# Forgetting attention: a hand-over to dense blocks before the values' product

## The chip, the cores and the metric

The kernel runs on one core of a Trainium2 chip. The metric is the device time of one execution in microseconds (us); lower is better. TensorE multiplies matrices, VectorE and ScalarE do elementwise work, GpSimd fills constants, and SyncE issues the transfers of weights from HBM.

## The reference, cut to what matters

A trunk of four layers over 272 positions (16 learned meta tokens and 256 real ones), model width 1024. Layers 0 and 3 mix tokens by forgetting attention, layer 1 by gated linear attention, layer 2 by a gated delta rule; each is followed by a dense SwiGLU network of inner width 2816. All inputs are float32. The forgetting attention has 16 heads of 64:

```python
def fox_attend(q, cq, qpos, k, v, ck, kpos):
    s = jnp.einsum('bqhd,bkhd->bhqk', q, k).astype(jnp.float32)
    bias = cq[..., :, None] - ck[..., None, :]
    mask = kpos[None, :] <= qpos[:, None]
    s = jnp.where(mask, s + bias, -jnp.inf)
    p = jax.nn.softmax(s, axis=-1)
    return jnp.einsum('bhqk,bkhd->bqhd', p.astype(v.dtype), v)
```

Its output is multiplied by a sigmoid gate and by an output matrix of 1024x1024.

## The kernel before

**Dense products.** Activations lie transposed, features on partitions and the 272 positions along the free axis. Every weight matrix is cut into blocks of 128x128, eight blocks to a unit of 128x1024. `make_unit` (line 573) loads a unit, lets ScalarE write its rounded high part `wh` and VectorE the rest `wl`. `block` (line 551) computes one block's share of an output as three matmuls in float32r: `zh,wh`, `zh,wl`, `zl,wh` (in the output projection `oh`, `ol`; in the dense network `ah`, `al`). An output of 128 features is a `Dense`, an accumulator in one of the eight PSUM banks; at most three are open while a mixer runs.

**The planner.** The order of all instructions is worked out while the program is built. `Trunk` keeps a clock of its own, `now`, advanced by estimated costs. Tasks are Python generators: a task that yields a tile, or a tuple of tiles, is taken up again when the plan's time of the last of these plus `LAT` (0.14 us) has come; one that yields an event waits until it is set; one that needs a PSUM bank asks for it every 0.1 us of the plan. `turn` (line 470) takes the first task that is due; if none is, `step` (line 506) places one dense block whose unit is split and whose accumulator is open. TensorE executes strictly in the order in which the planner placed its work. A matmul placed before its operands are there by the plan moves the plan's clock forward (line 403); on the chip the engine waits. The ScalarE and VectorE work has planned slots too, and is ordered by them. The plan halves TensorE's speed after a thin stretch; it looks at that in fixed ticks of its clock.

**Forgetting attention** (`fox`, line 828). Its dense outputs come in this order: the forget gate; then for each of four groups of two head pairs the queries, keys and values; then the eight gates. A generator `attend(jp)` (line 932) treats a pair of heads, `hh` = 0 and 1:

1. It waits for the scores' inputs and for the event of the pair before, and takes four banks (`pa`, `pb` for each head).
2. It places the bias product (`cs,sel`) and the scores (`raw`) in three tiles of queries (96, 96 and 80 positions), then the softmax on VectorE and ScalarE, which ends in the normalised `pr`.
3. It yields on `pr[0]`, transposes the first head's `pr` on TensorE (six transposes, `con,pr` in the rows, line 424) into a bank `pt` and a corner of `pb`, and copies them out: ScalarE writes `pts` (96x448), VectorE `pt2` (80x80). It yields on `pr[1]` and does the same for the second head.
4. It takes a bank `po` and places the values' product: `vsb` against `pts` and `pt2` of both heads, the two heads in different columns of the array. ScalarE copies `po` to `osb`.

There are 8 pairs in each of two layers, so 16 such products. In the rows digits at the end of a name are dropped, so `pt2` stands as `pt`. `gate_done` (line 1009) later multiplies `osb` by the gate and splits the result into `oh` and `ol` for the output projection. In the last layer the 16 meta positions are left out of it (`lo` = 16).

Of the kernel before, what the change touches and what calls it, by code (L numbers as in the profile page):

```python
# [308 lines left out]
class Trunk:  # L309
# [518 lines left out]
    def fox(self, j, lo, gain):  # L828
# [9 lines left out]
        with ExitStack() as cx:  # L838
# [93 lines left out]
            def attend(jp):  # L932
                yield cs_ev
                yield qk_ev[jp]
                yield v_ev[jp]
                if jp:
                    yield s_ev[jp - 1]
                cs = csx[0]
                qn, kn, vsb = raws[jp, 0], raws[jp, 1], vs[jp]
                pa0, pb0, pa1, pb1 = yield from self.bankn(4)  # L940
                pa, pb = (pa0, pa1), (pb0, pb1)
                R = [slice(64 * hh, 64 * hh + 64) for hh in range(2)]
                for hh in range(2):
                    r, hd = R[hh], 2 * jp + hh
                    self.mm(pa[hh][:96, :288], self.pick(r, hd, 96), cs[r, T : T + 288], True, False)
                    self.mm(pb[hh][:80, :T], self.pick(r, hd, 80), cs[r, :T], True, False)
                sm = [tp.tile([96, w], F32, tag="sm", name="sm") for _ in range(2)]
                pr = [tp.tile([96, w], F32, tag="pr", name="pr", bufs=4) for _ in range(2)]
                mn, su, ri = ([tp.tile([96, 3], F32, tag=t, name=t) for _ in range(2)] for t in ("mn", "su", "ri"))
                views = [[], []]  # L950
                for i3, (a, b) in enumerate(qt):
                    nq = b - a
                    for hh in range(2):
                        src = (pa[hh][:nq, 0:96], pa[hh][:nq, 96:288], pb[hh][:nq, :T])[i3]
                        self.mm(src, qn[R[hh], a:b], kn[R[hh], :b], False, i3 > 0)
                        views[hh].append((slice(0, nq), slice(offs[i3], offs[i3] + b), src))
                for hh in range(2):
                    for i3, (rows, cols, src) in enumerate(views[hh]):
                        v.tensor_tensor_reduce(sm[hh][rows, cols], src, mask[rows, cols], 1.0, BIG, ALU.add, ALU.min, mn[hh][rows, i3 : i3 + 1])
                    for i3, (rows, cols, src) in enumerate(views[hh]):  # L960
                        s.activation(pr[hh][rows, cols], sm[hh][rows, cols], AF.Exp, bias=mn[hh][rows, i3 : i3 + 1], scale=-1.0, accum_out=su[hh][rows, i3 : i3 + 1])
                    for i3, (rows, cols, src) in enumerate(views[hh]):
                        v.reciprocal(ri[hh][rows, i3 : i3 + 1], su[hh][rows, i3 : i3 + 1])
                        v.tensor_scalar(pr[hh][rows, cols], pr[hh][rows, cols], ri[hh][rows, i3 : i3 + 1], None, ALU.mult)
                self.free(pa0)
                self.free(pa1)
                self.set(s_ev[jp])
                yield pr[0]
                pts, pt2 = [], []
                for hh in range(2):  # L970
                    pt = yield from self.bank()
                    for i3, (a, b) in enumerate(qt):
                        for k3 in range(i3 + 1):
                            t0, n = TILES[k3]
                            src = pr[hh][: b - a, offs[i3] + t0 : offs[i3] + t0 + n]
                            if k3 == 0:
                                dst = pt[:n, a:b]
                            elif k3 == 1:
                                dst = pt[:n, T + a - 96 : T + b - 96]
                            else:  # L980
                                dst = pb[hh][:n, T : T + 80]
                            self.tr(dst, src)
                    x = tp.tile([96, 448], F32, tag="pts", name="pts")
                    x2 = tp.tile([80, 80], F32, tag="pt2", name="pt2")
                    s.activation(x[:, lo:], pt[:96, lo:448], AF.Copy)
                    v.tensor_copy(x2, pb[hh][:80, T : T + 80])
                    self.free(pt)
                    self.free(pb[hh])
                    pts.append(x)
                    pt2.append(x2)  # L990
                    if hh == 0:
                        yield pr[1]
                po = yield from self.bank()
                for i3 in range(3):
                    for hh in range(2):
                        r = R[hh]
                        if i3 == 0:
                            self.mm(po[r, lo:T], vsb[:96, 0, r], pts[hh][:, lo:T], True, False, 0.5)
                        elif i3 == 1:
                            self.mm(po[r, 96:T], vsb[:96, 1, r], pts[hh][:, T:448], False, False, 0.5)  # L1000
                        else:
                            self.mm(po[r, 192:T], vsb[:80, 2, r], pt2[hh], False, True, 0.5)
                s.activation(osb[:, jp, lo:], po[:, lo:T], AF.Copy, scale=0.5)
                self.free(po)
                self.set(o_ev[jp], osb[:, jp])
# [23 lines left out]
            for jp in range(KD):  # L1029
                self.dense(z, zev, KD, gate_done(jp), lo)  # L1030
                self.go(attend(jp))
# [825 lines left out]
```

## Time and profile before

| | |
|---|---|
| Median of 3 runs | 1552.88 us (1547.57 to 1555.5) |
| The profiled execution | 1550.78 us |
| Its span, first to last instruction | 1549.0 us |
| TensorE, matmuls busy | 1498.8 us (97%) |
| VectorE busy | 1092.3 us (71%) |
| ScalarE busy | 781.8 us (50%) |
| Mean granted TensorE clock | 0.983 of full speed |

The profiled execution is one run; its span leaves out what lies around the instructions. A matmul's duration in a row covers its passage through the array, and successive matmuls overlap, so the distance from one start to the next tells the pace. PE is TensorE's matmuls, PEld its weight loads, DVE VectorE, ACT ScalarE. L260, L419 and L424 are the helper lines through which every elementwise operation, every matmul and every transpose passes; operations are told apart by their tiles, as in `ps<-pts,vsb`.

### The profile page before, as it was taken

What the parts mean: (1) busy time and instruction counts of PE and PEld (TensorE: products, weight loads), DVE (VectorE), ACT (ScalarE), POOL (GpSimd) and SP (SyncE); (2) the same over time, 40 slices, a digit from 0 to 9 for tenths busy, and PEclk for the clock granted to TensorE, in tenths of its full rate; (3) what the DMA queues carried; (4) which work ended last, traced back from release to release, by engine and by line L of the source; (5) the groups of instructions that cost most, each with busy time, mean ns of one, the idle gap of its engine ahead of it and who ended that gap; (6) DMA issues with size and microseconds to landing.
All of it is one profiled execution on the core that took longest, in us unless ns stands there. A gap on an engine that the chain in (4) does not pass through costs nothing.

```text
span 1549.0 us, 29524 instructions
## 1 busy us (share of the span) xinstructions
PE 1498.8 (97%) x11985; PEld 1453.4 (94%) x11985; DVE 1092.3 (71%) x2161; ACT 781.8 (50%) x1418; POOL 18.1 (1%) x58
## 2 busy tenths in 40 slices
PE   7899999999999999999898998999999999999999
PEld 7888999999999999999897897999999888999999
DVE  7778776665796876655979476866656778786653
ACT  6556554444445544444675354544445556654442
POOL 0000000000000000000200000000000000000000
PEclk9999999999999999999998897999999999999999
DMA  5232455555433455555333021455554333455564
GB/s 192 98 107 96 156 178 175 177 177 177 145 102 106 144 187 168 175 178 175 112 122 109 21 86 65 161 178 172 177 172 163 110 111 108 136 191 189 184 199 138
DMA packets 63737, 225.25 MB, mean 145 GB/s; under 512 B 7232, under 2 KB 9632, under 8 KB 63600
## 3 DMA queue, kind: packets, MB, share of 16 engines
q1 hardware_dynamic: 63600, 223.36, 43.3%
q8 instruction: 94, 1.54, 0.4%
q14 instruction: 43, 0.35, 0.1%
HBM read 222.28 MB, written 1.05 MB: 144 GB/s over the span
## 4 chain that ended last, share of the span: by engine, by line
PE 82%; DVE 11%; ACT 4%; issue 1%; DMA 1%; SPq 0%; DVEq 0%; ACTq 0%
PE ps L419 82%; DVE wl L260 3%; ACT pr L260 1%; ACT wh L260 1%; DVE rq L260 1%; DMA w<-in_w_dram 1%; DVE pr L260 1%; DVE sm L260 1%; PE ps L424 1%; DVE k L260 1%; ACT pts L260 0%; DVE ri L260 0%; DVE yc L260 0%; SPq L392 0%; DVE d L260 0%
## 5 line engine op out<-in xcount | busy, mean ns | idle before, releaser
L419 PE MATMUL ps<-zh,wh 128*128 128x272 f32 (+1 forms) x2400 | 711.2, 296 | 8.2 <-ACT zh L260 6.8
L419 PE MATMUL ps<-zh,wl 128*128 128x272 f32 (+1 forms) x2400 | 693.4, 289 | 3.1 <-DVE wl L260 3.1
L419 PE MATMUL ps<-zl,wh 128*128 128x272 f32 (+1 forms) x2400 | 695.0, 290 | 0.0
L260 ACT ACTIVATE wh<-w 128x1024 fp32r<-128x1024 f32 x420 | 443.1, 1056 | 384.3 <-PE ps L419 191.6
L260 DVE TENSOR_TENSOR wl<-w,wh 128x1024 fp32r<-128x1024 f32 x420 | 512.2, 1221 | 161.4 <-ACT wh L260 161.1
L419 PEld LDWEIGHTS ps<-zh,wh 128*128 128x128 f32 x2400 | 456.6, 190 | 17.2 <-ACT zh L260 6.7
L419 PEld LDWEIGHTS ps<-zh,wl 128*128 128x128 f32 x2400 | 456.7, 190 | 6.0 <-DVE wl L260 4.4
L419 PEld LDWEIGHTS ps<-zl,wh 128*128 128x128 f32 x2400 | 456.3, 190 | 0.0
L419 PE MATMUL ps<-al,wh 128*128 128x272 f32 (+1 forms) x704 | 202.0, 287 | 0.0
L419 PE MATMUL ps<-ah,wl 128*128 128x272 f32 (+1 forms) x704 | 201.4, 286 | 0.0
L419 PE MATMUL ps<-ah,wh 128*128 128x272 f32 (+1 forms) x704 | 201.0, 285 | 0.0
L419 PEld LDWEIGHTS ps<-ah,wh 128*128 128x128 f32 x704 | 133.1, 189 | 0.0
L419 PEld LDWEIGHTS ps<-al,wh 128*128 128x128 f32 x704 | 132.4, 188 | 0.0
L419 PEld LDWEIGHTS ps<-ah,wl 128*128 128x128 f32 x704 | 132.2, 188 | 0.0
L260 DVE TENSOR_TENSOR s<-t,rs 128x272 f32<-128x272 f32 (+1 forms) x88 | 38.5, 437 | 64.9 <-ACT t L260 64.8
L260 DVE TENSOR_TENSOR al<-a,ah 128x272 fp32r<-128x272 f32 (+1 forms) x88 | 38.6, 438 | 64.4 <-ACT ah L260 64.3
L419 PE MATMUL ps<-oh,wh 128*128 128x272 f32 (+1 forms) x256 | 75.6, 295 | 1.2 <-ACT wh L260 1.2
L419 PE MATMUL ps<-oh,wl 128*128 128x272 f32 (+1 forms) x256 | 74.7, 292 | 1.0 <-DVE wl L260 0.9
L419 PE MATMUL ps<-ol,wh 128*128 128x272 f32 (+1 forms) x256 | 74.7, 292 | 0.1
L260 ACT ACTIVATE ah<-a 128x272 fp32r<-128x272 f32 (+1 forms) x88 | 36.8, 418 | 62.9 <-DVE a L260 62.9
L260 ACT ACTIVATE zh<-h,par 128x272 fp32r<-128x272 f32 x64 | 32.7, 519 | 67.7 <-DVE h L260 66.5
L260 ACT ACTIVATE pr<-sm,mn 96x192 f32<-96x192 f32 (+3 forms) x96 | 42.2, 441 | 26.3 <-DVE mn L260 26.2
(225 smaller groups left out, 1511.7 us busy)
## 6 DMA issues: line engine op xcount, KB each, us to landing
w<-in_w_dram SPq DMA_DIRECT2D x420, 512.0 KB, 3.3
h<-in_h_dram SPq DMA_DIRECT2D x4, 272.0 KB, 5.2
out_dram<-h SPq DMA_DIRECT2D x8, 128.0 KB, 3.3
mask<-in_fmask_dram SPq DMA_DIRECT2D x2, 210.0 KB, 5.0
con<-in_con_dram SPq DMA_DIRECT2D x1, 207.5 KB, 6.0
mask<-in_gmask_dram SPq DMA_DIRECT2D x1, 126.0 KB, 2.1
par<-in_par_dram SPq DMA_DIRECT2D x1, 87.5 KB, 3.1
half<-in_dmask_dram SPq DMA_DIRECT2D x1, 36.0 KB, 1.7
```

The lines of the kernel that those rows point to most:

```text
L260: r = f(*args, **kw)
L419: ins = self.nc.tensor.matmul(out, lhsT, rhs, start=start, stop=stop)
L424: ins = self.nc.tensor.transpose(out, in_, self.con("ident")[:n, :n])
```

## The change

One line goes into `attend`, between the copies of the second head and the request for the bank of the values' product: the generator yields on all four copies, so that it is taken up again only when the plan has the last of them done, and meanwhile other due tasks and dense blocks are placed.

```diff
@@ -990,6 +990,7 @@
                     pt2.append(x2)
                     if hh == 0:
                         yield pr[1]
+                yield tuple(pts + pt2)
                 po = yield from self.bank()
                 for i3 in range(3):
                     for hh in range(2):
```

## Rows read from the trace of the kernel before

**Rows 1.** The page: busy time of each engine; the chain by engine.
```profile
PE 1498.8 (97%) x11985; PEld 1453.4 (94%) x11985; DVE 1092.3 (71%) x2161; ACT 781.8 (50%) x1418; POOL 18.1 (1%) x58
...
PE 82%; DVE 11%; ACT 4%; issue 1%; DMA 1%; SPq 0%; DVEq 0%; ACTq 0%
```

**Rows 2.** Windows: stretch, length, busy time (instructions) of each engine, clock, DMA share, GB/s.
```profile
51.00:163.00 112.00, 105.95 (x854) 94.44 (x852) 83.45 (x275) 64.25 (x172) 0.00 (x0) 1.00 0.30 99
163.00:186.00 23.00, 23.00 (x186) 23.00 (x185) 17.84 (x30) 14.49 (x23) 1.18 (x2) 1.00 0.48 161
...
840.00:960.00 120.00, 116.02 (x929) 104.91 (x929) 73.80 (x177) 55.85 (x141) 1.00 (x10) 0.86 0.17 55
...
1218.00:1329.00 111.00, 105.77 (x867) 94.52 (x866) 84.23 (x280) 64.48 (x176) 0.00 (x0) 1.00 0.30 101
```

**Rows 3.** Waits of PEld over the span: who for whom, us in total, times, longest.
```profile
PEld ps L419 <- ACT pts L260: 15.6, 32, 1.8
...
PEld ps L424 <- DVE pr L260: 5.1, 16, 0.5
PEld ps L419 <- ACT sq L260: 4.6, 8, 1.0
```

**Rows 4.** The same waits in 83:86, 153.9:157.3 and 1320.7:1324, one row each.
```profile
PEld ps L419 <- ACT pts L260: 0.7, 2, 0.5
...
PEld ps L419 <- ACT pts L260: 1.8, 1, 1.8
...
PEld ps L419 <- ACT pts L260: 1.7, 1, 1.7
```

**Rows 5.** Timeline of PE, third pair: start, length, engine, operation, count, [idle before, releaser].
```profile
83.56 0.29 PE L419 MATMUL ps<-zl,wh 128*128 128x272 f32 x1
83.69 0.62 PE L424 MATMUL ps<-con,pr 96*96 96x96 f32 x6
84.59 1.10 PE L419 MATMUL ps<-pts,vsb 96*64 96x272 f32 x6 [0.28 <-ACT pts L260]
...
86.06 0.50 PE L419 MATMUL ps<-cs,sel 64*96 64x288 f32 x4
```

**Rows 6.** Timelines of ACT and DVE at the same pair.
```profile
83.07 1.04 ACT L260 ACTIVATE wh<-w 128x1024 fp32r<-128x1024 f32 x1
84.02 0.95 ACT L260 ACTIVATE pts<-ps 96x448 f32<-96x448 f32 x2
...
84.14 1.23 DVE L260 TENSOR_TENSOR wl<-w,wh 128x1024 fp32r<-128x1024 f32 x1 [0.24 <-ACT wh L260]
85.28 0.23 DVE L260 COPY pt<-ps 80x80 f32<-80x80 f32 x1
```

**Rows 7.** Tile `wl`, stretches 0:84.1 and 0:153.9: operation, count, duration, first and last start.
```profile
L419 PE MATMUL ps<-zh,wl x126: 282/288/428, 7.1 to 83.4; 128*128 128x272 f32 x126
L260 DVE TENSOR_TENSOR wl<-w,wh x17: 1206/1220/1226, 5.2 to 77.5; 128x1024 fp32r<-128x1024 f32 x17
...
L419 PE MATMUL ps<-zh,wl x238: 282/288/428, 7.1 to 153.8; 128*128 128x272 f32 x119
L260 DVE TENSOR_TENSOR wl<-w,wh x30: 1206/1221/1226, 5.2 to 144.6; 128x1024 fp32r<-128x1024 f32 x30
```

**Rows 8.** Timeline of PE at the seventh pair of layer 0.
```profile
153.91 0.29 PE L419 MATMUL ps<-zl,wh 128*128 128x272 f32 x1
154.13 0.67 PE L419 MATMUL ps<-pts,vsb 96*64 96x272 f32 x2
156.14 0.67 PE L419 MATMUL ps<-pts,vsb 96*64 96x272 f32 x4 [1.34 <-ACT pts L260]
```

**Rows 9.** Timelines of ACT and DVE at the seventh pair.
```profile
154.74 0.93 ACT L260 ACTIVATE oh<-og 128x272 fp32r<-128x272 f32 x2
155.57 0.52 ACT L260 ACTIVATE pts<-ps 96x448 f32<-96x448 f32 x1
...
155.56 1.22 DVE L260 TENSOR_TENSOR wl<-w,wh 128x1024 fp32r<-128x1024 f32 x1
```

## The prediction

> **What bounds the kernel now.** I read the page's busy line first, then its chain, then the windows by stage, then who TensorE waits for. TensorE is busy 97% of a span of 1549.0 us, and 82% of the chain that ended last is its matmuls [rows 1]. No other engine comes near: VectorE has 71%, ScalarE 50%. So microseconds count here only where TensorE stands still, or runs at its lower clock. A stretch of nothing but dense blocks shows its pace: 186 matmuls in 23.00 us, 0.124 us each, so a dense block of three takes 0.37 us [rows 2]. Both attention stretches (51 to 163 and 1218 to 1329) are less than full, with a granted clock of 1.00, that is 2.4 GHz: no time is lost to the clock there [rows 2].
>
> The table of waits then says for whom: TensorE's weight loads waited 15.6 us in all for the copies `pts`, 32 times, which is twice for each of the 16 head pairs (8 pairs in each of two attention layers) [rows 3]. That is the wait at which the change aims. One ordinary pair shows it step by step [rows 5]: the second head's six transposes start at 83.69 and last 0.62 us, the first matmul of the values' product starts only at 84.59, and the next pair's work at 86.06. ScalarE shows why: it is at a weight split (`wh`, 1.04 us from 83.07) and then makes both `pts` copies back to back, 0.95 us from 84.02; VectorE has a weight split of 1.23 us from 84.14 between its two small `pt2` copies, the last of which starts at 85.28 [rows 6]. The pair loses 0.7 us (the first row of [rows 4]).
>
> **The change, step by step.** It adds no instruction and removes none. It makes the planning generator hand over once per pair, until the plan's time for the last of the four copies plus 0.14 us, so that `turn` can place dense blocks there; before, `pe` just moved its clock to the operand's time and the real engine stood still.
>
> *What must be there to fill the hole.* From the end of the transposes to the last copy of the ordinary pair it is about 1.2 to 1.5 us (84.1 to 85.5) [rows 5, 6], so three or four blocks. By 84.1 VectorE had finished 17 weight splits, 8 blocks each, 136 blocks, and 126 had been used (one `wl` matmul per block): 10 blocks lay ready [rows 7]. The same count gives 9 to 12 at the other thirteen pairs of this kind. So 14 pairs have their filling; the plan can see it, since its rule for a block is only that the unit is split and an accumulator is open.
>
> *The two exceptions.* At the seventh pair of each layer the dense supply ran out: by 153.9, 30 splits make 240 blocks and 238 were used [rows 7]. There the product already gave way to blocks (through the wait for a PSUM bank), was then issued at 154.13, and stood from there to 156.14 for the second copy [rows 8], because ScalarE had four gate operations ahead of that copy, the last two of them `oh` from 154.74, and the copy came at 155.57; the next split `wl` began only at 155.56 [rows 9]. These two waits are 1.8 and 1.7 us [rows 4]. A yield has nothing to put there. Bounds: nothing to 3.5 us; I take nothing, as the two blocks that lay ready are nearer to that [rows 7].
>
> *The sum.* Fillable: 15.6 - 1.8 - 1.7 = 12.1 us in 14 pairs.
> Against it stands what is left where the plan wakes before the real copy is done. The trace has this for yields of the same form: 16 pairs yield twice for `pr` before transposing, and TensorE still lost 5.1 us over those 32 yields, 0.16 each [rows 3]. The dearer neighbour is `sq`: 0.6 us each time it did wait (4.6 us in 8) [rows 3]. I take 0.16, since it is the same generator a few lines earlier: 14 x 0.16 = 2.2 us. With 0.6 it would be 8.4.
> Then one more change from dense blocks to the product: from the last dense matmul at 153.91 to the product at 154.13 is 0.22 us against a pitch of 0.124, so 0.10 more [rows 8]; 14 x 0.10 = 1.4 us. Bounds nothing to 0.2 each.
> 12.1 - 2.2 - 1.4 = 8.5 us. Ends: 12.1 - 8.4 - 1.4 = 2.3, and all 15.6.
>
> The Trainium skill, "TensorEngine Tiling (Array Packing)", section "Key Properties", says that a change of tiling mode drains TensorE. That speaks against this change, which puts full-array blocks between the transposes and a product on 64 columns (96*64 in the rows). It gives no figure; the row's 0.10 us agrees in kind, and by the rule alone the sum would only be 8.5 less some such tenths.
>
> *What is moved past what.* The weights' DMAs are issued as blocks are placed, so three or four blocks per pair pull the next load and split forward by about that much; DMA share in the stage is 0.30 [rows 2], and their number is the same. On TensorE the product, and behind it the next pair's scores, now come up to a block (0.37 us) later than the copies: waiting for that are `osb` on ScalarE and the next pair's softmax. Nobody needs `osb` before the gate of its pair, and the gates are the last eight dense groups. For the last pair the cover is the full 23 us from 163 on [rows 2]. If the blocks pulled forward were missed later as cover of the next softmax, TensorE would wait for a split (1.23 us on VectorE [rows 6]); with 10 ready and VectorE at 83.45 of 112.00 us [rows 2], I cost this at nothing.
>
> *Where the rest of the stall goes.* What is late next in the pair is `pt2`, behind the weight split; the new wait includes it, and blocks cover it too.
>
> **The total.** The profiled execution took 1550.78 us (span 1549.0); 1550.78 - 8.5 = 1542.3. The median of the runs shown is 1552.88, 2.1 us higher, which gives 1544.4 on that footing. I take the value between, 1543.
>
> **Rivals.**
> *The stall comes back as leftover.* The plan's copies are earlier than the real ones, because ScalarE and VectorE have other work ahead of them that the plan puts slightly elsewhere, so each product still waits 0.6 us as for `sq`. For: ScalarE's `wh` right before the copies [rows 6]. Against: the 0.16 of `pr`. Gain 2.3 us: 1550. The sister case, that the plan believes the copies are there at once and yields nothing, gives 1552.
> *Everything fills, tail too.* With the hand-over at the seventh pair, the eighth's transposes, 12 in one run right behind that product, could go first, and splits come sooner. Gain 14 us or so: 1537. Against: the blocks were used up there [rows 7, 9].
> *Slower: the plan is dealt anew downstream.* Every later decision of the planner stands on its clock, which has fixed ticks and counts TensorE as slow after a thin one; a layer of attention that ends some microseconds sooner shifts all ticks for the two chunked mixers. The place is the third layer's solve, where the granted clock is 0.86 over 120 us: with levels of 1.2 and 2.4 GHz that is about 34 us at the lower one, costing some 17 us [rows 2]. If the new deal thins TensorE's work there, that stretch doubles: +17 - 8.5 = +8.5, 1561. It decides once about 33 us more run at 1.2 GHz. Against: the same blocks and tasks in nearly the same order; a thicker deal is as likely, and would give 1535. Beside this row stands the Trainium skill, "TensorE: Matmul & The Clock Gate", section "What's actually happening": the chip's activity window runs free of the kernel's start, so a shift alone can change which matmuls are caught. No row here shows a shift.
>
> **How the numbers follow.** A measurement can tell about 0.5% from no change, 7.8 us, so 1545.1 and 1560.6 are the edges. Forecast (1538 to 1547): 0.50, of which 0.40 lie below 1545.1. Everything fills, or a lucky deal: 0.13. Leftover: 0.25; nothing yielded: 0.04; slower: 0.08. Faster 0.53, same 0.10 + 0.25 + 0.04 = 0.39, slower 0.08. The range 1534 to 1552 takes in the forecast, the leftover and most of the full gain.
>
> **What the profile after would show.** Right: the wait of TensorE for `pts` falls from 15.6 to under 6 us, most of that at the seventh pairs; dense matmuls stand between the `con,pr` transposes and `pts,vsb`; the stretches from the first pair to the last become shorter by 4 us each; the clock in them stays at 1.00. Wrong: the wait for `pts` stays over 9 us (leftover), or it falls and the span doesn't (then look for a new wait for `wl` or `pr` in these stretches, and at the clock of the third layer's solve). The prediction fails as a whole if the middle layers differ by more than the attention stretches.

## The result and the profile after

The changed kernel took 1534.92 us (median of 4, 1533.96 to 1536.62), the kernel before beside it 1554.19 us (median of 4, 1547.57 to 1557.22). The ratio is 0.9883, 95% interval 0.9849 to 0.9917: 1.2% faster, about 18 us, where 0.64% of the first median had been forecast, 10 us. The direction was right. The time lies in the range of 1534 to 1552 by 0.9 us, but outside the 1538 to 1547 that was forecast: the gain is nearly twice the forecast.

The page of the changed kernel, engines and span (compare [rows 1]):

```profile
span 1534.8 us, 29515 instructions
...
PE 1490.3 (97%) x11985; PEld 1449.0 (94%) x11985; DVE 1092.2 (71%) x2161; ACT 780.1 (51%) x1418; POOL 18.1 (1%) x58
```

The same number of matmuls, 8.5 us less busy time of TensorE and 14.2 us less span. Its waits after (compare [rows 3]), columns us in total, times, longest:

```profile
PEld ps L419 <- DVE wl L260: 6.6, 10, 1.8
...
PEld ps L419 <- ACT sq L260: 6.0, 10, 1.3
...
PEld ps L424 <- DVE pr L260: 3.6, 12, 0.3
...
PEld ps L419 <- ACT pts L260: 1.2, 4, 0.4
```

The wait for `pts` went from 15.6 us to 1.2. Most of it was not turned into other waits: `sq` gained 1.4 and `wl` 0.8, `pr` lost 1.5. One more wait grew, which shows at the matmuls and not at the weight loads: that for the softmax (`mn`) to have read a bank of scores, `pa`, so that the bank is free. Before and after:

```profile
PE ps L419 <- DVE mn L260: 1.1, 2, 0.8
...
PE ps L419 <- DVE mn L260: 2.9, 4, 1.3
```

All of the 1.8 us more lie in layer 0.

Windows of the changed kernel, the stretches of [rows 2]:

```profile
51.00:163.00 112.00, 108.43 (x901) 98.33 (x900) 87.13 (x285) 67.43 (x181) 0.00 (x0) 1.00 0.32 104
...
840.00:960.00 120.00, 112.40 (x950) 102.19 (x949) 79.76 (x191) 57.97 (x146) 1.00 (x10) 0.93 0.18 60
...
1218.00:1329.00 111.00, 109.44 (x917) 100.43 (x916) 88.27 (x269) 66.69 (x171) 0.00 (x0) 1.00 0.35 115
```

In both attention stretches TensorE now does some 50 matmuls more in the same time. And a thing the change does not touch moved too: in layer 2 (840 to 960) the mean granted clock is 0.93 in place of 0.86.

A timeline of TensorE at the third pair shows what fills the hole (compare [rows 5]):

```profile
82.28 0.62 PE L424 MATMUL ps<-con,pr 96*96 96x96 f32 x6
82.70 0.37 PE L419 MATMUL ps<-zh,wh 128*128 128x272 f32 x1
...
83.25 0.50 PE L419 MATMUL ps<-cs,sel 64*96 64x288 f32 x4
83.58 1.12 PE L419 MATMUL ps<-raw 64*96 64x96 f32 x12
84.63 0.98 PE L419 MATMUL ps<-pts,vsb 96*64 96x272 f32 x8
85.44 0.31 PE L419 MATMUL ps<-pt,vsb 80*64 80x80 f32 x4
85.68 0.39 PE L419 MATMUL ps<-zh,wh 128*128 128x272 f32 x1
```

Behind the transposes comes one dense block, then the bias product and the scores of the next pair, and only then the values' product. That product is shorter too, 1.05 us from its start to the next work's, against 1.47 in [rows 5]: both heads' copies are there, so the two halves of the array run together from the start (the heads' first matmuls start at 84.63 and 84.64), where before the second head's first matmul started 0.43 us behind the first's. At the fourth pair, where no next pair was ready, four dense blocks stand there instead.

To see where the time went, I cut each trace at the same pieces of work. Each dense block has one matmul with `wl`, 3360 in all in order of time; a stretch runs from one numbered block to another. In us:

| stretch (blocks) | before | before, again | after | layer 0 only | layer 3 only | no next pair | shift only | dense first |
|---|---|---|---|---|---|---|---|---|
| layer 0 attention (40 to 280) | 149.6 | 149.1 | 143.3 | 143.5 | 152.1 | 140.2 | 152.1 | 139.7 |
| layer 1 (880 to 1080) | 116.3 | 115.9 | 116.4 | 116.4 | 116.3 | 127.7 | 116.4 | 116.5 |
| layer 2 (1680 to 2000) | 243.2 | 243.2 | 240.0 | 236.6 | 243.2 | 232.5 | 233.2 | 231.5 |
| layer 3 attention (2560 to 2800) | 140.7 | 140.7 | 134.2 | 140.7 | 134.3 | 132.7 | 140.7 | 132.6 |

After against before in the two profiles: -6.3, 0, -3.2 and -6.5. From block 280 to block 960, and through all the dense networks, the two traces keep their distance to 0.2 us. These sums are 1.8 us more than the 14.2 us of the span, mostly because block 40, ahead of all attention, came 1.6 us later in the profile after (28.0 us for 26.4); the ten profiles, whose order of TensorE's work is the same up to there, have it between 26.3 and 28.6 us.

### The profile page after: what moved, and what is told of

It reads as the page before. It is cut to its first block, busy times and chain, and to the rows that moved or that the text cites. A ratio compares the mean times of both kernels' runs of the same rounds, so it can differ in the third digit from the quotient of the medians.

```text
span 1534.8 us, 29515 instructions
## 1 busy us (share of the span) xinstructions
PE 1490.3 (97%) x11985; PEld 1449.0 (94%) x11985; DVE 1092.2 (71%) x2161; ACT 780.1 (51%) x1418; POOL 18.1 (1%) x58
## 3 DMA queue, kind: packets, MB, share of 16 engines
HBM read 222.28 MB, written 1.05 MB: 146 GB/s over the span
```

## The experiments

Two theories stood at the start. One: the gain is TensorE's lost waits in 16 pairs, half in each layer, and the rest is by the way. Two: a good part of it is layer 2, ordered anew behind a planner's clock that stands elsewhere.

**The hand-over in layer 0 alone.**

```diff
-                yield tuple(pts + pt2)
+                if j == 0:
+                    yield tuple(pts + pt2)
```

> The hand-over in the first layer alone. If the gain lies in the attention stretches (theory 1), TensorE's stretch from the first head pair to the output projection of layer 0 is 6.3 us shorter, layer 3's is as before, and the wait for pts that is left is layer 3's half, about 8 us. If the order of the third layer's work, dealt anew behind a shifted planner clock, gives a good part of the whole (theory 2), that part shows here in full, since everything ahead of layer 3 is ordered as in the changed kernel: the whole would be -9 to -13 us, against -6 if the middle gives nothing.

1539.02 us against 1551.16 (ratio 0.9929, 0.9904 to 0.9953), so -11 us. Of the wait for `pts` 7.6 us are left, nearly all of it layer 3's half. Layer 0's stretch is 5.6 to 6.1 us shorter, layer 3's as before, and layer 2's 6.6 us shorter. Theory two holds for this half: layer 2 gives about as much as the hand-over itself.

**The hand-over in layer 3 alone.**

```diff
-                yield tuple(pts + pt2)
+                if j == 1:
+                    yield tuple(pts + pt2)
```

> The hand-over in the last layer alone; the first three layers are ordered as in the kernel before. Theory 1: -6.5 us in layer 3's stretch and nothing elsewhere, so -6.5 in all. Theory 2: the same in the stretch, and the rest of the changed kernel's gain (about 19 by the medians, less 13 in the two stretches, so 6 us) is missing here and found in the run with layer 0 alone.

1543.95 us (ratio 0.9957, 0.9935 to 0.998), -6.7 us, and the stretch of layer 3 is 134.3 us: the clean price of the hand-over in one layer, with layers 1 and 2 ordered and timed as before. The two halves add up to the whole (-11 and -6.7 against -18).

This profile brought something that was not looked for. Its layer 0 is ordered as before, yet took 152.1 us, not 149.6. Windows of the first kernel's profile, then of this one, which lies 2 us later, so that the same work is compared:

```profile
150.20:157.20 7.00, 5.51 (x46) 4.52 (x43) 6.82 (x26) 5.41 (x15) 0.00 (x0) 1.00 0.00 0
157.20:164.10 6.90, 6.74 (x57) 6.15 (x57) 2.95 (x7) 3.66 (x8) 0.00 (x0) 1.00 0.51 154
```

```profile
152.20:159.20 7.00, 5.50 (x44) 4.51 (x44) 6.85 (x25) 5.32 (x15) 0.00 (x0) 1.00 0.00 0
159.20:166.10 6.90, 6.90 (x36) 5.95 (x34) 1.86 (x5) 2.04 (x5) 0.00 (x0) 0.51 0.50 154
```

The stretch that ends with the seventh pair's waits (TensorE busy 5.50 of 7.00 us) was followed in this execution by some 7 us at 0.51, the lower level of 1.2 GHz; 36 matmuls were done there instead of 57. Four profiles have the old order in layer 0; in two of them the clock fell behind those waits, in two it did not. In none of the six profiles with a hand-over in layer 0 did it fall. So in some executions the stretch lost 2.7 us more. That the waits are the cause is likely by their place; with two profiles of four against none of six it is not shown.

**The next pair kept out of the hole.** The event that admits the next pair is set behind the product.

```diff
-                self.set(s_ev[jp])
                 yield pr[0]
...
+                self.set(s_ev[jp])
                 s.activation(osb[:, jp, lo:], po[:, lo:T], AF.Copy, scale=0.5)
```

> The hand-over in both layers, but the event that lets the next pair start is set only when the values' product has been placed, so the next pair's scores can't fill the hole; dense blocks and the sums of squares can. If dense blocks are enough, as the prediction had it, the two stretches are as short as in the changed kernel (together 12.8 us shorter than before) and the wait for pts stays near 1.2 us. If the early scores matter, because the next pair's softmax starts earlier and its later waits shrink with it, the stretches gain only 8 to 10 us, and the wait for pr or sq is larger than in the changed kernel by the difference.

Neither: the stretches gain more, 9.1 and 8.0 us. The third pair of this kernel:

```profile
80.81 0.62 PE L424 MATMUL ps<-con,pr 96*96 96x96 f32 x6
81.23 0.38 PE L419 MATMUL ps<-zh,wh 128*128 128x272 f32 x1
...
82.71 0.29 PE L419 MATMUL ps<-zl,wh 128*128 128x272 f32 x1
82.92 0.98 PE L419 MATMUL ps<-pts,vsb 96*64 96x272 f32 x8
```

Four dense blocks fill the hole, as the prediction had drawn it, and the wait for `pr` is 1.1 us, for `pts` 0.2. The early scores do not help. A reason that the rows suggest, not tested by itself: with two pairs under way eight banks are short, and in the changed kernel TensorE waited 2.9 us, four times, for the softmax to read `pa` and so free a bank, where before it was 1.1; in this run that wait is gone from both stretches. By its size it could be two thirds of layer 0's further gain and about half of layer 3's.

The whole was 1533.82 us all the same (ratio 0.9882), since layer 1 lost 11 us: its order changed too. In that layer TensorE waited for a weight split, and then ran at the lower clock:

```profile
PEld ps L419 <- ACT wh L260: 5.5, 2, 4.0
...
455.00:468.00 13.00, 10.19 (x105) 9.77 (x104) 9.05 (x17) 6.14 (x14) 1.88 (x7) 1.00 0.24 83
468.00:482.00 14.00, 12.09 (x70) 11.48 (x71) 6.10 (x9) 7.47 (x13) 0.00 (x0) 0.51 0.36 114
```

**The kernel before, once more.**

> The kernel before once more, for a second profile of the same order of instructions. If the middle layers' time depends on where the clock falls and not on the order alone, the low-clock stretches from 750 to 970 us (51 us in the first profile) lie elsewhere or sum differently here, and the span differs by half of that difference; if the order alone sets them, they are the same within a window.

1551.33 us, and the stretches of layers 1 to 3 within 0.5 us of the first profile, the low-clock places of layer 2 within 1 us of their old ones. With this order layer 2 takes the same time again, 243.2 us in three profiles; with the changed kernel's order four profiles lie between 236.6 and 240.0 us, so the order sets it to within a few microseconds.

**The planner's clock alone.** No hand-over; one line in the dense network of layer 0 moves the clock by 2.70 us.

```diff
+            if gain == "g_mix1":
+                self.now += 2.70
```

> The kernel before, without the hand-over; the planner's clock alone is set 2.70 us forward once, in the dense network of layer 0. The attention of layer 0 is ordered as before, layer 1 too; layer 2 gets the order that the run without the next pair had. Theory: the place of the planner's fixed ticks alone decides the order of layer 2, and that order how long TensorE runs at 1.2 GHz there; the wait for pts stays at 15.6 us, both attention stretches are as long as before, and layer 2 is some 10.6 us shorter, as it was in that run (243.2 to 232.6 us from block 1680 to block 2000). Rival: layer 2 was shorter there because of where the chip's own clock windows fell, and here it is as before, no change in all.

1544.25 us against 1552.3 (ratio 0.9945, 0.9923 to 0.9967): -8.5 us without touching attention. The wait for `pts` stays at 15.3 us, layer 3's stretch at 140.7, and layer 2 is 233.2 us, 10.0 shorter, with the very order of TensorE's work that the run without the next pair has there (232.5 us). Programs that were only built, not run, close the circle: other shifts give other orders of layer 2, a shift by one whole tick of the planner gives back the old one, and a shift of 2.97 us, which puts the ticks where the hand-over in layer 0 puts them, gives TensorE the changed kernel's order of layer 2. So what the change won in layer 2 is owed to where the ticks fall. Windows from block 1840 to block 2000, before and then with the shift alone:

```profile
853.60:991.20 137.60, 131.97 (x1011) 120.57 (x1011) 89.91 (x199) 62.55 (x147) 0.40 (x4) 0.89 0.23 74
```

```profile
859.20:987.20 128.00, 123.60 (x1019) 114.39 (x1019) 89.57 (x200) 62.60 (x149) 0.50 (x5) 0.95 0.25 79
```

The same 160 blocks, at a mean clock of 0.95 for 0.89.

**Six pairs of eight in layer 3.**

```diff
-                yield tuple(pts + pt2)
+                if j == 0 or jp < 6:
+                    yield tuple(pts + pt2)
```

> The changed kernel, but in the last layer pairs seven and eight do not hand over; layers 0 to 2 are ordered as in the changed kernel. The prediction put nothing on these two pairs, where no split weights lay ready: then layer 3's stretch (block 2560 to 2800: before 140.7, changed 134.2 us) stays at 134.2. If the hand-over gains there through other work, above all the eighth pair's transposes, the stretch is 136 to 138 us and a wait for pts of about 2 us is back.

The stretch is 136.1 us: the last two pairs give 1.9 of layer 3's 6.5 us. In the whole 1538.32 us (ratio 0.9909). TensorE at the seventh pair, here and then in the changed kernel:

```profile
1309.65 0.65 PE L419 MATMUL ps<-pts,vsb 96*64 96x256 f32 x2
1311.52 0.65 PE L419 MATMUL ps<-pts,vsb 96*64 96x256 f32 x4 [1.23 <-ACT pts L260]
```

```profile
1308.64 1.06 PE L424 MATMUL ps<-con,pr 80*96 80x80 f32 x12
1310.03 1.23 PE L419 MATMUL ps<-pts,vsb 96*64 96x256 f32 x6
```

With the hand-over the eighth pair's transposes, and one dense block more, come ahead of the seventh's product, where without it the product is issued first and stands.

**Yielding on ScalarE's copies alone, in layer 3.**

```diff
-                yield tuple(pts + pt2)
+                yield tuple(pts + pt2) if j == 0 else tuple(pts)
```

> The changed kernel, but in the last layer the generator yields on ScalarE's two pts copies alone, not on VectorE's pt2, which come last. If the product needs pt2 late enough, or dense blocks cover either wait, layer 3's stretch is 134.2 us give or take 0.4. If pt2 is the wait that would come next, TensorE waits for it in some six pairs, some 0.3 us each, and the stretch is about 2 us longer.

134.4 us, the same. But this run says little: TensorE's order in that layer differs from the changed kernel's at one place only, the eighth pair's product, so at the other seven pairs nothing was tested. That `pt2` is no wait that comes next is shown by the changed kernel itself, in whose trace TensorE's weight loads never wait for it.

**Dense blocks first, with the ticks put back.** The kernel without the next pair, and the planner's clock moved by 0.60 us in the dense network of layer 0.

```diff
-                self.set(s_ev[jp])
                 yield pr[0]
...
+                self.set(s_ev[jp])
                 s.activation(osb[:, jp, lo:], po[:, lo:T], AF.Copy, scale=0.5)
...
+            if gain == "g_mix1":
+                self.now += 0.60
```

> The hand-over with the next pair let in only behind the product, and the planner's clock set 0.60 us forward once in the dense network of layer 0, so that layer 1 is ordered as in the kernel before and layer 2 as in the run without the next pair. If the three parts add up, attention of layer 0 gives -9.4, layer 2 -10.6 and attention of layer 3 -8.0: -28 us, 1523. If layer 1's loss of 11 us in the run without the next pair was no matter of its order but of what attention left behind, it comes back and the time is 1534.

1526.59 us against 1552.3 (ratio 0.9835, 0.9804 to 0.9866), faster than both kernels, by -26 us where -28 had been expected. Its stretches (last column of the table) are -9.6, 0, -11.7 and -8.1 us: layer 1's loss is gone with its order, and the parts add up.

## Why the prediction was right, and where it was off

**What bounds, and where the gain lies: right.** TensorE's own waits for `pts` were the thing to win; they fell from 15.6 to 1.2 us, and in layer 3, where little else moved, the stretch shrank by 6.5 us for 6.3 us of this wait lost. That the weights lay ready and that `pt2` would not become the bound held; waits for the splits `wl` grew by 0.7 us in layer 0 and by nothing in layer 3.

**The sum: too small, 8.5 against 12.5 us** (6.0 and 6.5 for the two layers, the first against the mean of the two undisturbed profiles of before). The term that was most mis-sized is the one put at nothing, the seventh pairs, since no split weights lay ready. What failed is "A yield has nothing to put there": it has the eighth pair's transposes, which the prediction named only as a rival. The run with six pairs gives 1.9 us for the last two pairs of layer 3, where the sum has 0.6 for the eighth alone, and 4.6 for the six before them, where the sum's 0.6 a pair makes 3.6. Layer 0 was not divided so.

Two terms were set against the gain. The leftover was put at 2.2 us after the price of `pr`; 1.2 us of `pts` is left over. And the change from blocks to the product was charged at 1.4 us. The row behind it is right, since the 0.21 us from a dense matmul to the product stands in the run without the next pair too (82.71 to 82.92 above). But it is hardly one change more: in the kernel's instructions the transposes, like the dense blocks, use the array whole (128x128), so before the change, too, every product came behind full-array work. In layer 3's stretch TensorE passes 29 times from one form of the array to another, before and after; in layer 0's it is 29 and 27 times. In layer 3 waits fell by 6.3 us (`pts`) and 0.7 (`pr`), `sq` rose by 0.3, and the stretch shrank by 6.5 of these 6.7 us. So no run here prices a change of form, and the rule that the prediction took from the Trainium skill ("TensorEngine Tiling (Array Packing)", "Key Properties") is neither borne out nor refuted.

One cost has no term in the sum: in layer 0, 8.0 us less wait for `pts` made the stretch only 6.0 us shorter, because the wait for `pa` rose by 1.8 us there, and those for `sq` and `wl` by 0.7 each.

**What fills the hole: half wrong.** The prediction had the next pair's scores come later, behind the product. In the first pair of each of the first three groups they come first, because `s_ev` is set before the transposes and four banks are free by the time the copies are awaited. The run that keeps them out shows that dense blocks alone do more, 3.1 us more in layer 0 and 1.5 in layer 3.

**The rival of the new deal: right in mechanism, open in sign, left out of the sum.** The prediction named the place (layer 2's solve, clock 0.86), the cause (a shift of the planner's ticks) and both signs, and gave the better deal a share of 0.13 with everything filling. It came out to the good, -3.2 us in the profile after and -4.4 to -6.6 in three more profiles with the same order, and makes a sixth to a third of the whole. Which way it went was luck: without it the time would lie, by these stretches, some 3 to 7 us higher, inside the forecast. The prediction's sign of failing as a whole, middle layers that differ by more than the attention stretches, did not come: at most 6.6 against 12.5 us. That the order does it, not where the chip's clock happens to stand, is shown by the shift alone and by the kernel before run again. By the trace's clock records, from block 1840 to block 2000, 30 us ran at 1.2 GHz before and 12 us after; half of the difference, 9 us, is somewhat over the 7.4 us by which that part shrank. The part ahead of it, from block 1680, went the other way, 29 us for 18 at the lower level, and is 4.2 us longer. What is left of the spread within one order has two parts. One is the clock: the profile after has some 10 us at the lower level around 770, where the other kernels with this order have 3.4. The other is waits: in one place TensorE stood for the tile `rr`, 3.5 us in the run with layer 0 alone, 4.1 in the profile after, and 5.5 in the runs with six pairs and with ScalarE's copies alone.

**The clock in attention: wrong as a rule.** "No time is lost to the clock there" was true of the one profile that was read. In two of four with the old order it was lost, 2.7 us, right behind the seventh pair's waits (in layer 0 0.4 us of wait for `pts` is left after the change).

Together: 6.0 to 8.6 us in layer 0, 3 to 7 in layer 2, 6.5 in layer 3, which spans the measured 18.

## What to carry to other kernels

Where one engine is the bound and runs in a fixed order, an unplanned wait of half a microsecond to two, 16 times, is worth nearly its full length as long as other work lies ready and no other resource, here the banks, runs short for it (6.5 us for 6.3 in layer 3, 6.0 for 8.0 in layer 0); count that work before pricing the hand-over, tasks as well as blocks, and look at which of them gets in first. A planner whose decisions hang on an absolute clock makes every edit an edit of all that follows: price the stages behind by what they spend at the lower clock, and separate the two with an experiment that moves the clock alone. And read the clock in more than one execution before saying that a stage loses nothing to it.

## What the runs showed of the hardware

Short waits, none above 1.8 us, strung over a stretch of 7 us in which TensorE was busy 5.50 us, were followed in some executions by some 7 us at 1.2 GHz and in others by none, with the same instructions in the same order. In layer 2 the order decided most of it: the same low-clock places came back within 1 us in the repeated kernel. Reordering one layer's work, with the same number of matmuls and of VectorE and ScalarE instructions, made layer 2 10.0 us shorter in one run (mean granted clock 0.95 for 0.89 in its second half) and layer 1 11.4 us longer in another, where 14 us ran at 0.51.
